# Two pieces of a recurrence unit, emitted level by level in turn

## The chip, the cores and the metric

The kernel runs on one core of one Trainium2 chip. The metric is the device time of one execution in microseconds (us). The engines are PE (TensorE, matrix products), PEld (its weight loads), DVE (VectorE), ACT (ScalarE), POOL (GpSimd) and SP (SyncE, which issues most transfers). Each engine takes its own instructions strictly in the order in which the built program lists them.

## The reference

A two-layer backbone over 2048 latent tokens and 256 context tokens of width 1024. Layer 0 is a neighbourhood attention, layer 1 a bidirectional gated linear recurrence with 8 heads of width 128. The change lies in layer 1:

```python
q, i_lat, f_fwd, f_bwd, g = jnp.split(h @ w_in, 5, axis=-1)
def step(S, inp):                                  # one chunk of tokens, per head
    A = jnp.cumsum(ac, axis=2)                     # running log decay
    o_inter = einsum('bhtk,bhkv->bhtv', qc * exp(A), S)
    scores = einsum('bhtk,bhsk,bhtsk->bhts', qc, kc, exp(rel))
    o_intra = einsum('bhts,bhsv->bhtv', scores, vc)
    S_new = exp(A_last)[..., None] * S + einsum('bhsk,bhsv->bhkv', kc * exp(A_last - A), vc)
x = x + gate * hgrn_readout(o_f + o_b, g, head_norm_w, w_out)
```

All of it is in float32 and is done for both directions, the latent scans starting from the context's final state.

## The kernel before, in words

Layer 1 has the 2048 tokens in four pieces of 512. Two pieces are resident at a time as transposed, normalised activations (`h1h`, `h1l`): pieces 0 and 1 first, then 2 and 3. A *unit* is one head on one pair of pieces, so there are 16 units: `first[0..7]` with pieces 0 and 1 (and the context), `second[0..7]` with pieces 2 and 3.

Every unit has two sections. `products` multiplies the activations with five weight granules: two forget gates, values, queries and the output gate. A granule is loaded (`g_raw`), split on ACT into `g_wh` (line 64) and on POOL into `g_wl` (line 67), and for each piece 24 matmuls of 512 columns go to one PSUM tile `g_ps` (lines 208 to 210); the context has 24 of 256 columns.

`rest` then calls `heavy` once for each piece. `heavy` computes the chunk scores with a tree of 7 levels, of blocks of 1, 2, 4, ..., 64 tokens. A first clump of 8 matmuls uses the sum of both directions' keys (`ksum`, line 918 on POOL). In each of levels 0 to 5 ACT copies the mixed keys to `km` (line 926), PE does 8 matmuls of 64 by 64 (line 914, tile `lv`; each is two passes in the trace, so 16 rows), DVE puts the result into `pm` under a mask (line 928, COPY_PREDICATED). Then `level_up` multiplies the keys (line 871), the queries (line 875) and the totals `F` (line 876) on DVE, which the next level reads. Level 6 has its own 8 matmuls (lines 933 and 934). After the levels comes the tail of the piece: transposed keys (`trp`, line 857), states (`u_ps`, line 884), outputs (`o_ps`, lines 949 and 952) with a chain of four state updates on DVE (line 954), and three stores on POOL's queue (`s_lo`, `s_lq`, `s_lu`, lines 964 to 969). `light` later walks the backward states of a second unit over all four pieces (lines 981 to 1008), reading those stores back.

In `rest` the two pieces of a unit are emitted one after the other: all levels and the tail of the first, then those of the second. The text of the program is not the order on the engines: a scheduler places the instructions of each engine by priority (what was emitted earlier goes first) and by when its model of the engines thinks that operands and buffers are there. So the levels of one unit end up between the `g_ps` products of the next unit. The helper `run` takes generators and advances them in turn until all have ended. The pieces share the score tiles' PSUM banks (`lv`, 2), the `km` buffers (2), one PSUM bank `o` for outputs and one buffer `op` for what is stored.

At the seam, `build` makes the activations of pieces 2 and 3 (lines 1047 to 1079). At the end, the last unit's `rest(2, 3)` comes before its gate granule (48 matmuls), and then `layer1_out` projects the result (`y_ps`).

Of the kernel before, what the change touches and what calls it, by code (L numbers as in the profile page):

```python
# [44 lines left out]
def custom(ap, dims, off=0):  # L45
    return bass.AP(tensor=ap.tensor, offset=ap.offset + off, ap=[list(ap.ap[0])] + dims)


class Core:
# [855 lines left out]
    def heavy(self, hd, piece, f2, k2, q2, q, v, wk, pp, sp, scale, kept, o_tag):  # L905
        nc, S = self.nc, self.S
        T = 512

        def scores(kt, qv):
            ps = pp.tile([P, 4, 64], F32, name="lv", tag="lv")  # L910
            for c in range(4):
                for u in range(2):
                    o = c * P + u * 64
                    nc.tensor.matmul(ps[64 * u:64 * u + 64, c, :], kt[:, o:o + 64], qv(o, u), start=True, stop=True)  # L914
            return ps
        pm = wk.tile([P, 4, 64], F32, name="pm", tag="pm")
        ksum = wk.tile([P, T], F32, name="ksum", tag="km")
        nc.gpsimd.tensor_add(ksum, k2[:, 0, :], k2[:, 1, :])
        ps = scores(ksum, lambda o, u: q[:, o:o + 64])
        nc.scalar.mul(out=pm, in_=ps, mul=scale)  # L920
        tot = f2
        for j in range(7):
            b = 1 << j
            if b < 64:
                km = wk.tile([P, T], F32, name="km", tag="km")
                nc.scalar.copy(out=km.rearrange("p (k h i) -> p k h i", h=2, i=b), in_=self.mixed(k2, T, b))  # L926
                ps = scores(km, lambda o, u: custom(q2, [[2 * b, 32 // b], [T + b, 2], [1, b]], o))
                nc.vector.copy_predicated(pm, self.masks[:, j, :].unsqueeze(1).broadcast_to([P, 4, 64]), ps)  # L928
            else:
                ps = pp.tile([P, 4, 64], F32, name="lv", tag="lv")  # L930
                for c in range(4):
                    o = c * P
                    nc.tensor.matmul(ps[0:64, c, :], k2[:, 0, o:o + 64], q2[:, 1, o + 64:o + P], start=True, stop=True)
                    nc.tensor.matmul(ps[64:P, c, :], k2[:, 1, o + 64:o + P], q2[:, 0, o:o + 64], start=True, stop=True)  # L934
                p = wk.tile([P, 4, P], F32, name="pf", tag="pf")
                nc.scalar.copy(out=p[0:64, :, 64:P], in_=ps[0:64])
                nc.scalar.copy(out=p[64:P, :, 0:64], in_=ps[64:P])
                nc.gpsimd.tensor_copy(p[0:64, :, 0:64], pm[0:64])
                nc.gpsimd.tensor_copy(p[64:P, :, 64:P], pm[64:P])
            nxt = self.totals(wk, T, j + 1, "F") if j < 6 else self.totals(sp, T, 7, "F")  # L940
            self.level_up(T, b, tot, k2, q2, nxt)
            tot = nxt
        nc.gpsimd.tensor_copy(self.fb[:, hd, piece, :], tot[:, 1, :])
        uf = self.states_in(k2, v, T, 0, wk, pp)
        o_ps = pp.tile([P, 4, P], F32, name="o_ps", tag=o_tag)
        s = self.sf[:, hd, :]
        last = None
        for c in range(4):
            m = nc.tensor.matmul(o_ps[:, c, :], p[:, c, :], v[:, c, :], start=True, stop=False)
            if last is not None:  # L950
                self.after(m, last)
            last = nc.tensor.matmul(o_ps[:, c, :], q2[:, 1, c * P:(c + 1) * P], s, start=False, stop=True)
            new = sp.tile([P, P], F32, name="s", tag="s") if c < 3 else self.sf[:, hd, :]
            nc.vector.scalar_tensor_tensor(new, s, tot[:, 0, c:c + 1], uf[:, c, :], ALU.mult, ALU.add)
            s = new
        if kept is None:
            op = wk.tile([P, 4, P], F32, name="op", tag="op", bufs=1)
        else:
            op, us = (kept[:, i].rearrange("p (c t) -> p c t", c=4) for i in range(2))
        nc.scalar.copy(out=op, in_=o_ps)  # L960
        if kept is not None:
            nc.scalar.copy(out=us, in_=self.states_in(k2, v, T, 1, wk, pp))
            return
        nc.gpsimd.dma_start(out=S["lo"][hd, piece], in_=op)
        nc.gpsimd.dma_start(out=S["lq"][hd, piece], in_=q2[:, 0, :])
        ub = self.states_in(k2, v, T, 1, wk, pp)
        us = wk.tile([P, 4, P], F32, name="us", tag="op", bufs=1)
        nc.scalar.copy(out=us, in_=ub)
        nc.gpsimd.dma_start(out=S["lu"][hd, piece], in_=us)
# [41 lines left out]
    def layer1(self, h1, hpool, gp):  # L1011
        nc, tc, I, S = self.nc, self.tc, self.I, self.S
        scale = float(P) ** -0.5
        with ExitStack() as st:
            wk = st.enter_context(tc.tile_pool(name="gk", bufs=2, reuse_waits="tile"))
            sp = st.enter_context(tc.tile_pool(name="gs", bufs=4, reuse_waits="tile"))
# [6 lines left out]
            pp = Banks()  # L1023
# [56 lines left out]
            class Unit:  # L1080
# [53 lines left out]
                    granule(32 + un.hd, pieces, un.o_g, nc.gpsimd if len(pieces) > 1 else nc.vector)  # L1134

                def rest(un, *pieces, o_tag="o"):
                    for g in pieces:
                        both = None
                        if un.keep:
                            both = wk.tile([P, 2, 512], F32, name="both", tag="k2", bufs=4)  # L1140
                            un.kept.setdefault(g, [None] * 3)[:2] = un.q2[g][:, 0, :], both
                        self.heavy(un.hd, g, un.f2[g], un.k2[g], un.q2[g], un.q[g], un.v[g], wk, pp, sp, scale, both, o_tag)

                def light(un, o_tag="o"):
                    return self.light(un.hd, wk, pp, sp, sm, un.kept, o_tag)
# [9 lines left out]
            def run(*work):  # L1155

                work = list(work)
                while work:
                    work = [w for w in work if next(w, work) is not work]
# [176 lines left out]
```

## Time and profile before

| | us |
|---|---|
| median of 3 runs (3338.64 to 3343.32) | 3340.88 |
| the profiled execution, its own time | 3345.1 |
| its span (first to last instruction) | 3343.3 |
| PE busy | 3211.4 |
| DVE busy | 1938.3 |
| ACT busy | 1137.0 |
| POOL busy | 842.8 |

Layer 1 begins at about 1710 us; the recurrence's clumps `lv` run from 1754.7 us to 3134 us. How to read it: busy time counts computing instructions alone. Matmuls are pipelined, so a row of the timeline gives a start and a duration, and the time that a matmul costs in a dense stream is the distance from its start to the next start, not its duration. Idle time in brackets stands in front of the instruction that waited, with what released it.

### The profile page before, as it was taken

To read this page: it belongs to the slowest core of one execution; us is meant where nothing else is said; L and a number is where in the kernel's file an instruction comes from. 1 tells how busy PE (TensorE), PEld (TensorE's weight loads), DVE (VectorE), ACT (ScalarE), POOL (GpSimd) and SP (SyncE) were. 2 spreads that over 40 slices of the span, in tenths; PEclk is the share of its full clock that TensorE was granted. 3 is DMA by queue.
4 is the path that set the end of the run, shared out by engine and by line. 5 is a ranking of instruction groups with operands and counts; after the bars stand their busy time and mean duration, and the time that the engine had idled before them with its cause. 6 is when DMAs were issued, how large, how long until landed. Compare 5 with 4: busy or idle time off the path is not lost. (4 is left out here: it accounts for less than half of the span.)

```text
span 3343.3 us, 58063 instructions
## 1 busy us (share of the span) xinstructions
PE 3211.4 (96%) x22988; PEld 2671.5 (80%) x22988; DVE 1938.3 (58%) x4002; ACT 1137.0 (34%) x2361; POOL 842.8 (25%) x813
## 2 busy tenths in 40 slices
PE   7999999999998998999999999999899999999798
PEld 4778889989787777778888888888688777887687
DVE  7674111111276776767536555565775677777776
ACT  3311110110254555553123333333533444444421
POOL 2210110110022322353322222222442323232321
PEclk8999999999999999999999999999999999999899
DMA  6566231332477767644321111112322333333543
GB/s 231 173 213 196 95 100 62 100 101 88 145 207 198 203 198 202 183 147 139 133 82 48 52 57 53 52 58 86 98 87 82 111 111 119 119 117 103 167 145 111
DMA packets 231048, 415.24 MB, mean 124 GB/s; under 512 B 35020, under 2 KB 110828, under 8 KB 230776
## 3 DMA queue, kind: packets, MB, share of 16 engines
q1 hardware_dynamic: 206904, 344.22, 33.7%
q0 software_dynamic: 23872, 67.31, 5.9%
q8 instruction: 182, 2.98, 0.4%
q14 instruction: 90, 0.74, 0.1%
HBM read 285.78 MB, written 127.10 MB: 123 GB/s over the span
## 5 line engine op out<-in xcount | busy, mean ns | idle before, releaser
L208 PE MATMUL g_ps<-h1h,g_wh 128*128 128x512 f32 x1280 | 513.9, 401 | 5.1 <-DVE qt L1094 2.5
L210 PE MATMUL g_ps<-h1h,g_wl 128*128 128x512 f32 x1280 | 511.6, 400 | 0.0
L209 PE MATMUL g_ps<-h1l,g_wh 128*128 128x512 f32 x1280 | 510.5, 399 | 0.0
L209 PE MATMUL mm<-lo,wh 128*128 128x512 f32 (+1 forms) x960 | 354.6, 370 | 1.2 <-DVE lo L202 1.0
L210 PE MATMUL mm<-hi,wl 128*128 128x512 f32 (+1 forms) x960 | 353.1, 369 | 1.3 <-POOL wl L67 1.3
L208 PE MATMUL mm<-hi,wh 128*128 128x512 f32 (+1 forms) x960 | 350.1, 371 | 1.6 <-DVE st L263 0.6
L586 DVE CUSTOM_DVE_ANT_0 p<-s,tab 128x768 f32<-128x768 f32 (+2 forms) x288 | 230.3, 836 | 122.1 <-PE s L580 101.6
L208 PEld LDWEIGHTS g_ps<-h1h,g_wh 128*128 128x128 f32 x1280 | 242.1, 189 | 56.7 <-DVE qt L1094 2.8
L210 PEld LDWEIGHTS g_ps<-h1h,g_wl 128*128 128x128 f32 x1280 | 242.2, 189 | 51.8
L67 POOL TENSOR_TENSOR g_wl<-g_raw,g_wh 128x1024 fp32r<-128x1024 f32 x86 | 209.7, 2438 | 290.7 <-ACT g_wh L64 277.8
L209 PEld LDWEIGHTS g_ps<-h1l,g_wh 128*128 128x128 f32 x1280 | 242.3, 189 | 49.2
L587 ACT ACTIVATE p<-p,nm 128x768 f32<-128x768 f32 (+2 forms) x288 | 239.8, 835 | 56.2 <-DVE nm L586 55.4
L928 DVE COPY_PREDICATED pm<-masks,lv 128x256 f32<-128x256 int32 x192 | 85.6, 446 | 262.8 <-PE lv L914 262.6
L208 PEld LDWEIGHTS mm<-hi,wh 128*128 128x128 f32 x960 | 179.8, 189 | 37.0 <-issue 2.6
L210 PEld LDWEIGHTS mm<-hi,wl 128*128 128x128 f32 x960 | 181.1, 189 | 32.3 <-POOL wl L67 1.8
L209 PEld LDWEIGHTS mm<-lo,wh 128*128 128x128 f32 x960 | 181.3, 189 | 32.1 <-DVE lo L202 2.4
L601 PE MATMUL tps<-ident,p 128*128 128x128 f32 x1472 | 198.9, 284 | 0.0
L67 POOL TENSOR_TENSOR wl<-wraw,wh 128x1024 fp32r<-128x1024 f32 x24 | 57.8, 2408 | 539.8 <-ACT wh L64 516.1
L871 DVE TENSOR_TENSOR k<-k,F 128x512 f32<-128x512 f32 (+1 forms) x240 | 165.6, 692 | 40.3 <-PE lv L934 35.6
L926 ACT COPY km<-k 128x512 f32<-128x512 f32 x192 | 129.1, 673 | 164.7 <-PE lv L914 146.0
L875 DVE TENSOR_TENSOR q<-q,F 128x512 f32<-128x512 f32 x192 | 184.6, 962 | 0.0
L601 PEld LDWEIGHTS tps<-ident,p 128*128 128x128 f32 x1472 | 164.1, 144 | 20.2 <-issue 1.5
(267 smaller groups left out, 6808.6 us busy)
## 6 DMA issues: line engine op xcount, KB each, us to landing
g_raw<-in_w SPq DMA_DIRECT2D x90, 512.0 KB
wraw<-in_w SPq DMA_DIRECT2D x32, 512.0 KB
s_q<-st SPq DMA_DIRECT2D x32, 512.0 KB
s_k<-st SPq DMA_DIRECT2D x32, 512.0 KB
adaw<-in_ada_w SPq DMA_DIRECT2D x64, 256.0 KB
q<-s_q SPq DMA_DIRECT2D x32, 512.0 KB
vb<-s_v SPq DMA_DIRECT2D x128, 128.0 KB
k<-s_k SPq DMA_DIRECT2D x16, 768.0 KB
```

The costliest lines, as they stand in the source:

```text
L67: e_lo.tensor_sub(lo, src, hi.bitcast(F32))
L208: nc.tensor.matmul(ps, wh(dc), hh(dc), start=dc == 0, stop=False)
L209: nc.tensor.matmul(ps, wh(dc), hl(dc), start=False, stop=False)
L210: m = nc.tensor.matmul(ps, wl(dc), hh(dc), start=False, stop=dc == n - 1)
L586: nc.vector.tensor_tensor_reduce(p[:, :n], s[a][:, 512 - nk:768], t, 1.0, 3.0e38, ALU.add, ALU.min, nm)
L587: core.exp = nc.scalar.activation(p[:, :n], p[:, :n], AF.Exp, bias=nm, scale=-1.0, accum_out=R.sums[:, a, j:j + 1])
L601: pin(nc.tensor.transpose(ps[:, i, :], self.p[a][:, c * P:(c + 1) * P], ident))
L871: nc.vector.tensor_mul(kv, kv, kf)
L875: nc.vector.tensor_mul(qv, qv, qf)
L926: nc.scalar.copy(out=km.rearrange("p (k h i) -> p k h i", h=2, i=b), in_=self.mixed(k2, T, b))
L928: nc.vector.copy_predicated(pm, self.masks[:, j, :].unsqueeze(1).broadcast_to([P, 4, 64]), ps)
```

## The change

`heavy` becomes a generator that yields in each level, after the level's scores are masked into `pm` and before `level_up`. `rest` makes one generator for each piece and gives them to `run`, so that level 0 of the first piece is emitted, then level 0 of the second, then `level_up` and level 1 of the first, and so on; the two tails follow at the end, first piece first. With one piece in `rest` nothing is interleaved. No instruction is added or left out. All later line numbers move by 1 and, from `rest` on, by 4.

```diff
@@ heavy
             nxt = self.totals(wk, T, j + 1, "F") if j < 6 else self.totals(sp, T, 7, "F")
+            yield
             self.level_up(T, b, tot, k2, q2, nxt)
@@ rest
+
+                    work = []
                     for g in pieces:
...
-                        self.heavy(un.hd, g, un.f2[g], un.k2[g], un.q2[g], un.q[g], un.v[g], wk, pp, sp, scale, both, o_tag)
+                        work.append(self.heavy(un.hd, g, un.f2[g], un.k2[g], un.q2[g], un.q[g], un.v[g], wk, pp, sp, scale, both, o_tag))
+                    run(*work)
```

PE, in the middle of the first eight units, before. `q_19905` are the queries of piece 0 of one unit, `q_19937` those of its piece 1; `g_ps` are products of the next unit:

```order
L208 MATMUL g_ps<-h1h,g_wh 128x512
L209 MATMUL g_ps<-h1l,g_wh 128x512
L210 MATMUL g_ps<-h1h,g_wl 128x512
L884 MATMUL u_ps<-t_v,t_kT 128x128 x2
L857 MATMUL trp<-ident,k_19530 128x128 x2
L914 MATMUL lv<-q_19905,km 64x64 x8
L208 MATMUL g_ps<-h1h,g_wh 128x512
L209 MATMUL g_ps<-h1l,g_wh 128x512
```

One level of one piece stands alone among the products here. The same unit in the changed program:

```order
L208 MATMUL g_ps<-h1h,g_wh 128x512
L209 MATMUL g_ps<-h1l,g_wh 128x512
L210 MATMUL g_ps<-h1h,g_wl 128x512
L208 MATMUL g_ps<-h1h,g_wh 128x512
L914 MATMUL lv<-q_19905,km 64x64 x8
L914 MATMUL lv<-q_19937,km 64x64 x8
L209 MATMUL g_ps<-h1l,g_wh 128x512
L210 MATMUL g_ps<-h1h,g_wl 128x512
L208 MATMUL g_ps<-h1h,g_wh 128x512
```

The clump of piece 1 has moved up beside the clump of piece 0: one interruption of the products in place of two.

DVE, the same unit, before: the level of one piece (mask, queries, keys) and between the levels work of the next unit.

```order
L928 COPY_PREDICATED pm<-masks,lv 128x256
L875 TENSOR_TENSOR q_19905<-q_19905,F_20029 128x128x2x2
L1109 TENSOR_TENSOR sgg<-g_ps,sgg 128x512
L871 TENSOR_TENSOR k_19532<-k_19532,F_20061 128x32x2x8
L928 COPY_PREDICATED pm<-masks,lv 128x256
L875 TENSOR_TENSOR q_19905<-q_19905,F_20045 128x64x2x4
```

DVE at the same levels, in the changed program:

```order
L928 COPY_PREDICATED pm<-masks,lv 128x256
L875 TENSOR_TENSOR q_19905<-q_19905,F_20029 128x128x2x2
L928 COPY_PREDICATED pm<-masks,lv 128x256
L875 TENSOR_TENSOR q_19937<-q_19937,F_20055 128x128x2x2
L871 TENSOR_TENSOR k_19532<-k_19532,F_20071 128x64x2x4
L871 TENSOR_TENSOR k_19534<-k_19534,F_20087 128x64x2x4
```

DVE now does both pieces' steps of a level in one group before the next pair of clumps can run.

PE near the end of layer 1, in the changed program: levels of the last unit (`q_30207` piece 2, `q_30239` piece 3) with the tail of the unit before it (`q_29315`) between them. In the old program this stretch holds levels of piece 2 alone, and those of piece 3 come later, among the last gate products.

```order
L914 MATMUL lv<-q_30239,km 64x64 x8
L884 MATMUL u_ps<-t_v,t_kT 128x128 x4
L914 MATMUL lv<-q_30207,km 64x64 x8
L857 MATMUL trp<-ident,k_29075 128x128 x4
L914 MATMUL lv<-q_30239,km 64x64 x8
L884 MATMUL u_ps<-t_v,t_kT 128x128 x4
L953 MATMUL o_ps<-s,q_29315 128x128
L950 MATMUL o_ps<-t_v,pf 128x128
L914 MATMUL lv<-q_30207,km 64x64 x8
```

All levels of the last unit now come ahead of its 48 gate products, and both pieces' tails come behind these.

## Rows read from the trace of the kernel before

**Rows 1.** The page's first part: busy time, share of the span, instructions.

```profile
PE 3211.4 (96%) x22988; PEld 2671.5 (80%) x22988; DVE 1938.3 (58%) x4002; ACT 1137.0 (34%) x2361; POOL 842.8 (25%) x813
```

**Rows 2.** Busy time by stretch: length, PE, PEld, DVE, ACT, POOL, granted clock, DMA.

```profile
1755.00:2340.00 585.00, 579.56 (x4428) 482.38 (x4425) 343.69 (x652) 202.40 (x376) 152.82 (x137) 1.00 0.18 58
2340.00:2460.00 120.00, 105.11 (x728) 84.90 (x727) 93.12 (x136) 60.00 (x101) 55.31 (x43) 0.94 0.30 92
2460.00:3071.50 611.50, 600.80 (x4386) 489.44 (x4385) 426.20 (x977) 256.00 (x618) 179.61 (x170) 0.99 0.34 107
3071.50:3143.90 72.40, 55.66 (x546) 46.79 (x545) 60.12 (x114) 34.19 (x73) 26.61 (x22) 0.88 0.47 151
```

**Rows 3.** Timeline of PE: start, duration, instruction; one clump among products.

```profile
2343.02 0.39 PE L210 MATMUL g_ps<-h1h,g_wl 128*128 128x512 f32 x1
2343.34 0.69 PE L914 MATMUL lv<-q,km 128*64 128x64 f32 x16
2343.96 0.50 PE L208 MATMUL g_ps<-h1h,g_wh 128*128 128x512 f32 x1
2344.29 0.39 PE L209 MATMUL g_ps<-h1l,g_wh 128*128 128x512 f32 x1
2344.52 0.40 PE L210 MATMUL g_ps<-h1h,g_wl 128*128 128x512 f32 x1
```

**Rows 4.** Timeline of PE, two clumps side by side among products.

```profile
1961.54 0.39 PE L209 MATMUL g_ps<-h1l,g_wh 128*128 128x512 f32 x1
1961.86 0.27 PE L933 MATMUL lv<-q,k 128*64 128x64 f32 x1
...
1962.38 0.64 PE L914 MATMUL lv<-qt,ksum 128*64 128x64 f32 x16
1962.94 0.50 PE L210 MATMUL g_ps<-h1h,g_wl 128*128 128x512 f32 x1
1963.28 0.39 PE L208 MATMUL g_ps<-h1h,g_wh 128*128 128x512 f32 x1
```

**Rows 5.** Timeline of PE, ten passes of 128 columns among products.

```profile
2004.06 0.39 PE L208 MATMUL g_ps<-h1h,g_wh 128*128 128x512 f32 x1
2004.28 0.38 PE L949 MATMUL o_ps<-t_v,pf 128*128 128x128 f32 x2
...
2005.31 0.48 PE L209 MATMUL g_ps<-h1l,g_wh 128*128 128x512 f32 x1
2005.62 0.39 PE L210 MATMUL g_ps<-h1h,g_wl 128*128 128x512 f32 x1
```

**Rows 6.** Groups of DVE, 1755 to 2340 us: count, busy, mean ns, idle before.

```profile
L875 DVE TENSOR_TENSOR q<-q,F 128x512 f32<-128x512 f32 x80 | 82.5, 1031 | 0.0
L871 DVE TENSOR_TENSOR k<-k,F 128x512 f32<-128x512 f32 x81 | 61.9, 764 | 13.7 <-PE lv L934 12.4 <-ACT km L926 1.3
L928 DVE COPY_PREDICATED pm<-masks,lv 128x256 f32<-128x256 int32 x81 | 36.3, 448 | 159.5 <-PE lv L914 159.5
```

**Rows 7.** Line 875 on DVE, 1755 to 2340 us: ns min/median/max.

```profile
L875 DVE TENSOR_TENSOR q<-q,F x80: 672/681/2925, 1762.9 to 2338.1; 128x512 f32<-128x512 f32 x80
```

**Rows 8.** Timeline of DVE and, in the second fence line, of POOL.

```profile
2338.14 2.92 DVE L875 TENSOR_TENSOR q<-q,F 128x512 f32<-128x512 f32 x1
2338.12 2.40 POOL L67 TENSOR_TENSOR g_wl<-g_raw,g_wh 128x1024 fp32r<-128x1024 f32 x1 [0.89 <-ACT g_wh L64]
```

**Rows 9.** Groups of POOL, 1755 to 2340, then 2460 to 3071.5 us.

```profile
L67 POOL TENSOR_TENSOR g_wl<-g_raw,g_wh 128x1024 fp32r<-128x1024 f32 x34 | 83.2, 2446 | 126.9 <-ACT g_wh L64 121.7 <-PE g_ps L210 4.9
L67 POOL TENSOR_TENSOR g_wl<-g_raw,g_wh 128x1024 fp32r<-128x1024 f32 x37 | 89.6, 2422 | 118.3 <-ACT g_wh L64 115.8 <-PE o_ps L952 2.3
```

**Rows 10.** Waits of PE, 2340 to 2460 us: total us, times, longest.

```profile
PE lv L914 <- DVE brs L174: 5.5, 1, 5.5
PE lv L933 <- DVE q L875: 4.2, 1, 4.2
```

**Rows 11.** Waits of PE, 3071.5 to 3143.9 us.

```profile
PE lv L914 <- DVE q L875: 5.1, 4, 2.1
PE lv L914 <- DVE rq_t L172: 2.7, 1, 2.7
```

**Rows 12.** What ACT waited for ahead of line 968, whole trace: us, times.

```profile
DMA s_lo<-op: 34.7, 19
```

## Prediction, made before the changed kernel ran

> **What bounds the kernel now.** I read the page's busy times first, then the busy time by stretch of layer 1, then PE's waits in the stretches where it idles, and last PE's timeline at a few clumps. The reader is to see that PE is the bound: it is busy 96% of the span [rows 1], and between 1755 and 2340 us, where the first eight units run, 579.56 of 585 us, with DVE at 344 and ACT at 202 [rows 2]. Only 5.4 us of that stretch, and 10.7 us of the 611.5 between 2460 and 3071.5, are PE idle. So there a better order can gain little by ending waits; it can gain only if PE's own stream gets shorter. PE does idle at the seam where pieces 2 and 3 are built (14.9 of 120 us) and at the end of layer 1 (16.7 of 72.4 us) [rows 2]. At the end DVE, with 60.1 of 72.4 us, is nearer its limit than PE.
>
> **What a clump costs PE.** Products follow each other at 0.23 us (2344.29 to 2344.52). From the last product before a lone clump to the second product behind it 1.27 us pass (2343.02 to 2344.29); two product steps would be 0.46, so a lone clump of 16 passes costs 0.81 us [rows 3]. A double clump of 32 passes takes 1.74 us between the same points (1961.54 to 1963.28), so it costs 1.28 us [rows 4]. Two lone clumps cost 1.62, and **joining two saves 0.34 us** of PE's time. It is paid in three places: the first pass starts 0.32 us after the last product and not 0.23, the first product starts late, and the second product 0.33 us after the first.
>
> It is the change to 64 columns that is dear, not any change of work: ten passes of 128 columns put among products take 1.56 us from product to second product (2004.06 to 2005.62); less two product steps that is 1.10 us, or 0.11 a pass, and nothing for the change [rows 5]. So I count clumps of `lv`, not all changes of work. The Trainium skill, "TensorEngine Tiling (Array Packing)", section Key Properties, says that changing the tiling mode, not merely the tile, drains TensorE. By that rule every entry to and exit from a 128 by 64 clump pays and a move between the 128 by 128 kinds does not, which is what these rows show; a sum over all changes of work would count twice as many as pay.
>
> **How many are joined.** The order of PE's instructions in the two programs gives the runs of `lv` matmuls that nothing interrupts. From the first clump to the first transposes of the seam there are 112 before and 63 now; in the seam 12 and 12; from there to the end of the last unit's products 132 and 123; after that 16 and 13. In the second half the walk over the backward states (`light`) cuts pairs apart again, hence the small change.
>
> **The change part by part**, against the profiled execution's 3345.1 us (span 3343.3):
>
> - First half: 49 joined × 0.34 = 16.7 us less on an engine that is 99% busy.
> - Second half: 9 × 0.34 = 3.1 us less.
> - New waits in these two halves. PE now needs both pieces' steps at one point. A pair needs 2 × (1.03 + 0.76 + 0.45) = 4.5 us of DVE, by means that hold DVE's delays already [rows 6]; in the place shown 21 products stand between two pairs, 4.8 us, and the pair itself takes 1.1. That covers it, with 1.4 us to spare, but before the change one piece's 2.2 us stood against about as many products. What else DVE does, 56% overall [rows 2], falls in part into the same interval. Bounds: 0, as now, up to the 39 us of the slower rival below. I take 5 us, a third more than the 16 us of idle time that the two stretches have, because the means of DVE stay under the interval.
> - Tails. In the old order the tail of the first piece was spread among the second piece's levels; now both tails follow each other: `op` has one buffer, so the copies and stores of the two pieces form one chain, store by store. ACT already waits for `s_lo`, 34.7 us in 19 times, 1.8 us each [rows 12], and key copies stand behind that wait. 15 units have both pieces here and one more such wait each: 15 × 1.8 = 27 us of ACT at most, off PE's path as long as products stand behind it. ACT is 35% busy [rows 2]; I add nothing and leave the bound to the range. SP's and POOL's transfers keep their number; each store moves with its tail.
> - The seam. Its two long waits are a level of the last first-half unit that stands behind the chain of the new pieces' normalisation on DVE (5.5 us) and a level-6 clump (4.2 us) [rows 10]. In the new order all levels of that last interleaved unit are ahead of the transposes, but the next unit's first level takes such a place. Bounds 0 and 9.7 us; I take 4.
> - The end. Before, no products stand in 3071.5 to 3103.5 us, 32 us, in which piece 2 of the last unit does its seven levels; then 40.4 us with 48 gate products and piece 3's levels, with waits of 5.1 and 2.7 us in the whole [rows 11]. Now both pieces do 14 levels in the first part. Its DVE work is 14 × 2.2 = 31 us by the means, and the tail of the unit before some 9 us more, so 40 us (8 more). The second part is then 48 × 0.23 = 11 us of products and two tails, about 13 us by what stands between 3131 and 3143.9 now: 24 us, 16 less. Together 8 less. Bounds: 0, and 16, since DVE's 60 us [rows 2] less some 4 us (two or three of its level steps now run earlier) have to fit.
>
> Sum: −16.7 − 3.1 + 5 − 4 − 8 = −26.8 us, 3318.3 us for the profiled execution. That execution is 4.2 us above the median of the runs, 3340.88; so **3314 us** in the measure of the runs.
>
> **The rivals.**
>
> 1. *DVE is held by POOL, and the change is slower.* A query step on DVE takes 0.68 us in the median and up to 2.93 [rows 7]; the one at 2338.14 took 2.92 us while POOL's 2.40 us subtraction for a granule ran from 2338.12 [rows 8]. There are 34 and 37 of these subtractions in the two halves [rows 9]. Until now such a hold hit one piece with a spare of 2 to 3 us before its next clump; now it pushes both pieces of a pair, whose spare is 1.4 us, and PE stands in front of the pair with its products queued behind. It costs PE about 1 us when it hits a pair's steps in full. The saving of 31.8 us is used up from 0.45 us for each of the 71; at 0.55, or 39 us, the sum is +7: **3348 us**, slower. For it: PE cannot pass the pair. Against it: the interval of 5.9 us is above the 4.5 us that already include the mean hold. The Trainium skill, "SBUF — State Buffer", section "SBUF: two separate sides", states that DVE and GpSimd share a port pair by an exclusive lock held for a whole instruction. By that rule the hold cannot be shared away and every subtraction that overlaps a pair costs in full; the 2.92 us row agrees.
> 2. *Waits eat the joined clumps; no change.* The same place at about 0.4 us for each subtraction, or the ACT waits of the tails at their bound of 27 us: the sum is within 6 us of zero, **3340 us**.
> 3. *Only the clumps count.* At the seam the wait merely changes its owner, and at the end 14 uncovered levels take as long as before in all: −16.7 − 3.1 + 5 = −14.8, **3326 us**. For it: at the end DVE is the nearer limit, and its work does not shrink.
>
> That the order does not change is excluded by the order itself: 49 pairs stand side by side in the first half.
>
> **How the numbers follow.** Forecast 60% (its own range 3298 to 3329); only the clumps 18%; no change 13%; slower 9%. What a measurement of this kernel can tell from no change is 0.2%, 6.7 us: below 3334.2 is faster, above 3347.6 slower. Faster 0.78, same 0.13, slower 0.09. The range from 3296 to 3336 leaves out the slower rival, about half of the no-change one and a twentieth below, where the end gains all of its 16 us and the seam all of its 9.7.
>
> **What would show it.** In the changed profile PE's busy time in the first half's stretch should fall by about 17 us with idle still under 10; double clumps of 32 passes should stand among products at 1.28 us each. The row of the end should be some 64 us long and the seam's two long waits smaller. DVE's, ACT's and POOL's busy times should stay. I am wrong if the first half is as long as before, with `lv` waiting for `q` some 20 us more; then the pairs wait, and rival 1 or 2 holds. I am wrong in size if the joined clumps do not take 1.28 us, or if the end stays at 72 us.

## The result, and the profile after

The changed kernel takes **3304.74 us** in the median (3296.95 to 3306.53, 4 runs) against 3340.15 for the kernel before in the same set; the ratio is 0.9884, with a 95% interval from 0.9869 to 0.9900. The forecast was 3314, in a range of 3296 to 3336. The sign and the cause of the largest term came out as forecast. The second half, the seam and the projection gained more than forecast and the end lost where a gain was forecast, and these misses partly offset each other.

The profiled execution took 3304.15 us, 41.0 less than the one before. Of that 6.1 us lie ahead of layer 1: its first product starts at 1682.75 instead of 1688.86. In layer 0 the two traces run within some 1.5 us of each other up to about 0.9 ms; behind that the distance comes and goes with PE's waits in the attention (between 1000 and 1600 us 14.3 us in one and 8.2 in the other for `q<-s_q`, but 10.1 and 16.9 for `ot`). Over all profiled executions of this study that start lies between 1679.2 and 1693.6 us, so it says nothing on the change, and all that follows counts from it. From there to the start of the last `y_ps` it is 1644.5 us before and 1609.7 now: 34.9 less, which is what the medians say (35.4).

Busy time by stretch in the changed kernel, cut at the same instructions as [rows 2], with the projection `y_ps` as a fifth row. Columns as there.

```profile
1748.89:2320.28 571.39, 560.96 (x4452) 475.33 (x4449) 333.71 (x652) 202.46 (x375) 154.97 (x135) 1.00 0.17 59
2320.28:2430.10 109.82, 102.64 (x704) 83.88 (x703) 86.06 (x136) 60.95 (x103) 55.91 (x45) 1.00 0.32 106
2430.10:3031.00 600.90, 593.79 (x4420) 486.67 (x4419) 426.54 (x974) 253.51 (x616) 182.41 (x173) 1.00 0.34 109
3031.00:3107.00 76.00, 57.76 (x522) 49.65 (x521) 52.09 (x121) 34.42 (x84) 19.88 (x18) 0.85 0.43 137
3107.00:3292.60 185.60, 182.41 (x822) 149.97 (x821) 144.31 (x357) 50.91 (x128) 45.28 (x19) 1.00 0.43 146
```

Length by length: 585.0 to 571.4 us (PE busy 18.6 us less, idle 5.0 more), 120.0 to 109.8, 611.5 to 600.9, but the end 72.4 to 76.0. The projection's stretch of before is a row that was not shown:

```profile
3143.90:3333.60 189.70, 184.47 (x832) 152.36 (x831) 141.34 (x361) 50.36 (x134) 41.26 (x18) 0.98 0.41 139
```

A joined pair in the first half, on PE's timeline of the changed kernel. The clump has the shape of [rows 4], from one more place:

```profile
1948.61 0.39 PE L210 MATMUL g_ps<-h1h,g_wl 128*128 128x512 f32 x1
1948.93 1.15 PE L914 MATMUL lv<-q,km 128*64 128x64 f32 x32
1950.01 0.50 PE L208 MATMUL g_ps<-h1h,g_wh 128*128 128x512 f32 x1
1950.35 0.39 PE L209 MATMUL g_ps<-h1l,g_wh 128*128 128x512 f32 x1
```

From 1948.61 to 1950.35 it is 1.74 us; less two product steps, 1.28 us, the forecast's price to the hundredth. There is one entry and one exit for the 32 passes of both pieces.

PE's waits in the first half (1748.89 to 2320.28) of the changed kernel: total us, times, longest.

```profile
PE lv L933 <- DVE q L875: 6.9, 5, 1.4
PE trp L857 <- ACT vT L850: 2.4, 5, 0.5
PE trp L857 <- DVE k L871: 1.1, 1, 1.1
```

The `km` levels (line 914) wait for nothing; before, it was 0.4 us once. Only level 6 (line 933) waits, five times. It uses keys and queries straight from `level_up`, without ACT's copy between; whether that is why was not tested.

The end shows the one new long wait. PE, then DVE, then POOL and SP, in the changed kernel around 3060 us; idle time ahead of an instruction stands in brackets:

```profile
3062.51 0.60 PE L857 MATMUL trp<-ident,vT 128*128 128x128 f32 x4
3070.21 2.45 PE L989 MATMUL o_ps<-s,box 128*128 128x128 f32 x8 [7.11 <-DVE s L992]
3072.31 0.78 PE L208 MATMUL g_ps<-h1h,g_wh 128*128 128x512 f32 x1
```

```profile
3059.98 0.88 DVE L875 TENSOR_TENSOR q<-q,F 128x512 f32<-128x512 f32 x1
3069.80 0.35 DVE L992 SCALAR_TENSOR_TENSOR s<-sb,fb,box 128x128 f32<-128x128 f32 x1 [8.94 <-DMA box<-s_lu]
```

```profile
3064.67 0.54 POOL L970 DMA_DIRECT2D s_lu<-us  x1 [2.70 <-ACT us L969]
3067.23 0.32 SPq L984 DMA_DIRECT2D box<-s_lu  x1
```

```profile
3061.43 0.54 POOL L965 DMA_DIRECT2D s_lo<-op  x1 [0.31 <-ACT op L961]
3063.73 0.32 SPq L985 DMA_DIRECT2D box<-s_lo  x1
3063.79 0.59 ACT L969 COPY us<-u_ps 128x512 f32<-128x512 f32 x1
```

Line 989 is the backward walk of unit 6. Its first state step on DVE (line 992) reads the states that this unit's second tail stored: the store is issued at 3064.67, the load at 3067.23, and the step starts at 3069.80. That is 5.1 us from store to use, while all levels of the last unit are done (DVE's last ended at 3060.9) and its 48 gate products stand on PE behind the walk. The last fence shows what stands ahead of the store: the outputs of the same tail are stored first, from the one `op` buffer that `us` takes next, and the copy into `us` starts as the load that follows that store is issued.

The Trainium skill, "SBUF — State Buffer", section "The DMA setup-cost knee", fits the time of a transfer by about 2 us and its bytes at 436 GB/s, and calls the fit an approximation. By that page the 256 KB store and the load that waits for it take 2.6 us each, an estimate of 5.2 us; the trace agrees with 5.1, of which 2.56 lie between the two issues.

### The profile page after: what moved, and what is told of

Read it like the earlier page. It is cut to its first block, busy times and chain, and to the rows that moved or that the text cites. A ratio compares the mean times of both kernels' runs of the same rounds, so it can differ in the third digit from the quotient of the medians.

```text
span 3302.3 us, 58252 instructions
## 1 busy us (share of the span) xinstructions
PE 3178.0 (96%) x22988; PEld 2657.8 (80%) x22988; DVE 1916.1 (58%) x4002; ACT 1136.8 (34%) x2361; POOL 845.6 (26%) x813
## 5 line engine op out<-in xcount | busy, mean ns | idle before, releaser
L208 PEld LDWEIGHTS g_ps<-h1h,g_wh 128*128 128x128 f32 x1280 | 241.2, 188 | 49.8 <-DVE hf L1076 0.6
L208 PE MATMUL mmv<-vh,hi 128*128 128x256 f32 x576 | 163.0, 283 | 0.0
L209 PE MATMUL mmv<-vl,hi 128*128 128x256 f32 x576 | 163.0, 283 | 0.0
L210 PE MATMUL mmv<-vh,lo 128*128 128x256 f32 x576 | 163.0, 283 | 0.0
```

Of the source, the lines that this page charges most:

```text
L208: nc.tensor.matmul(ps, wh(dc), hh(dc), start=dc == 0, stop=False)
L209: nc.tensor.matmul(ps, wh(dc), hl(dc), start=False, stop=False)
L210: m = nc.tensor.matmul(ps, wl(dc), hh(dc), start=False, stop=dc == n - 1)
```

## The experiments

The table gives the stage lengths of every profiled execution in us, each the difference of two starts on PE's timeline: first `lv` to the seam's first transpose; to its last; to the last product ahead of the last gate; to the first `y_ps`; to the last `y_ps`. The seam's cuts lie 25 us behind the first and 20 us ahead of the second of those in [rows 2]. The sixth column adds the last two stages, the seventh runs from layer 1's first product to the last `y_ps`.

| | first half | seam | second half | end | `y_ps` | end + `y_ps` | layer 1 |
|---|---|---|---|---|---|---|---|
| before | 610.3 | 75.0 | 631.4 | 72.6 | 189.5 | 262.1 | 1644.5 |
| changed | 592.8 | 68.5 | 620.9 | 76.2 | 185.4 | 261.6 | 1609.7 |
| e1_first | 592.8 | 68.5 | 629.1 | 73.9 | 189.6 | 263.5 | 1619.7 |
| e2_second | 611.0 | 73.7 | 619.4 | 69.8 | 186.0 | 255.9 | 1625.8 |
| e3_last | 610.7 | 75.1 | 631.7 | 70.2 | 188.4 | 258.6 | 1641.9 |
| e4_not_last | 592.7 | 68.5 | 619.8 | 70.0 | 189.1 | 259.1 | 1605.9 |
| e5_gate_early | 592.7 | 68.5 | 619.8 | 84.6 | 182.3 | 266.9 | 1613.7 |
| e6_light_late | 592.7 | 69.4 | 617.6 | 84.5 | 180.4 | 264.9 | 1610.3 |
| e10_l6_o | 593.1 | 68.7 | 618.2 | 75.9 | 202.5 | 278.4 | 1624.3 |
| e13_notlast_l6o | 593.0 | 68.5 | 619.5 | 78.6 | 197.4 | 276.0 | 1622.8 |
| e14_other | 592.9 | 68.6 | 621.5 | 64.5 | 188.7 | 253.2 | 1602.0 |
| e16_usfirst | 592.5 | 72.8 | 617.5 | 62.4 | 186.5 | 248.9 | 1597.6 |
| e17_usfirst6 | 592.9 | 68.5 | 617.8 | 67.8 | 189.9 | 257.7 | 1602.8 |
| e18_usfirst6_notlast | 592.8 | 68.5 | 619.5 | 68.2 | 190.6 | 258.8 | 1605.4 |

The first half repeats within 0.6 us over all of those that share its edit, so its gain is known well. The second half repeats less well: nine kernels have the very same order of PE's instructions there (the changed one, e4 to e14, e17 and e18) and take 617.6 to 621.5 us. Of the last two stages there are only two runs with nearly the old kernel's order, which differ by 1.4 us in their sum.

**Which stage gains.** Four kernels apply the change to some units only, by a condition in `rest`:

```diff
-                    run(*work)
+                    if 0 in pieces:
+                        run(*work)
+                    else:
+                        for w in work:
+                            run(w)
```

This is e1_first; e2_second has `2 in pieces and not un.keep`, e3_last `un.keep`, e4_not_last `not un.keep`.

> Only the units of the first half (pieces 0 and 1) have their two pieces' levels in turn; the second half and the last unit go piece by piece as before. PE's order is that of the changed kernel through the seam, and behind it that of the kernel before. Theory A (each stage has its own gain, and what it gains stays): the first half is 17 us shorter with 49 joined clumps and the seam 6 us, so 23 to 24 us less than before, 3317. Theory B (the gain of the first half is only shifted, and the second half, bound by its own waits, gives part of it back): less than 15 us.

Measured: 3318.81 us against 3341.6, ratio 0.9922 (0.9909 to 0.9936), 22.8 us less. The first half is 17.5 us shorter and the seam 6.5, and the second half does not give it back. Theory A holds.

> Only units 0 to 6 of the second half have their levels in turn; the first half and the last unit go piece by piece. The prediction's own price (9 clumps less of lv at 0.34 us, and idle time about as before) gives 3 us less than before. Theory A, from the changed kernel's stage times (631.4 to 620.9 us between the seam and the last products): 10 us less, 3330, since what counts is how often PE changes between lv and any other work, products above all, and idle time of PE falls by 4 us too.

Measured: 3326.18 us, ratio 0.9950 (0.9937 to 0.9962), 15.4 us less. The second half is 12.0 us shorter: theory A, and not the forecast's 3 us. The end and the projection are 6.2 us shorter too, which neither expected.

> Only the last unit has its levels in turn. The prediction's step for the end: 8 us less than before, all of it between the last products of the unit and the first y_ps. Theory A: nothing gained, within 2 us of before, or some us more: with both pieces' levels done early, nothing is left for PE while the backward walk waits for the stored states of the unit before, and the gate products stand behind that walk.

Measured: 3338.30 us, ratio 0.9989 (0.9981 to 0.9998); the last two stages are 3.5 us shorter. The forecast's 8 us are not there; theory A's bound of 2 us is passed as well. So the last unit alone does gain something when the unit before it goes piece by piece.

> All units but the last have their levels in turn; the last goes piece by piece. The prediction's step for the end: 8 us slower than the changed kernel, 3313. Theory A (the end gains nothing by the change, and piece 3's levels still cover the wait for the stored states): as long as the changed kernel or up to 5 us shorter, 3300 to 3305.

Measured: 3303.46 us, ratio 0.9887 (0.9872 to 0.9902). To leave the last unit out costs nothing, where the forecast's step would have cost 8 us. In this kernel the stored states are waited for by DVE for 1.7 us instead of 8.9, since piece 3's levels stand there, and PE's wait ahead of the walk is short:

```profile
3068.89 0.54 POOL L970 DMA_DIRECT2D s_lu<-us  x1 [3.72 <-ACT us L969]
3074.26 0.35 DVE L992 SCALAR_TENSOR_TENSOR s<-sb,fb,box 128x128 f32<-128x128 f32 x1 [1.68 <-DMA box<-s_lu]
```

```profile
PE o_ps L989 <- DVE s L992: 0.8, 1, 0.8
```

The first row is POOL's timeline, the second DVE's, the third PE's waits between the last products and the first `y_ps`. From store to use it is 5.4 us here too: as long as in the changed kernel, but covered.

**Can other work fill the wait?** Three kernels move the gate products or the walk.

```diff
 e5_gate_early
+            second[7].gate(2, 3)
             next(l6), next(l6)
             second[7].rest(2, 3)
-            second[7].gate(2, 3)
             next(l6), next(l6)
 e6_light_late
-            next(l6), next(l6)
             second[7].rest(2, 3)
             second[7].gate(2, 3)
-            next(l6), next(l6)
+            next(l6), next(l6), next(l6), next(l6)
 e10_l6_o
-            l6, l7 = second[6].light("mm"), second[7].light()
+            l6, l7 = second[6].light(), second[7].light()
```

> The changed kernel, with the last unit's 48 gate products emitted ahead of the backward walk of the unit before; in PE's order they stand ahead of all but the first of the last unit's levels. Round-trip theory (in the changed kernel PE waits 7.1 us at that walk for states that were stored only 5 us before, with the gate products queued behind): the wait falls under the levels, and the products fill PE's gaps ahead of it; but nothing is then left for the tails. 5 us less than the changed kernel, 3300. Rival (the end is bound by DVE's level steps): same as the changed kernel within 2 us, since the levels only start later.

Measured: 3304.93 us, ratio 0.9899 (0.9885 to 0.9912): no gain, and by the trace the last two stages are 5.3 us longer than in the changed kernel. The walk's wait falls to 4.9 us in three, but levels without products beside them now wait, 9.1 us in six (`lv` for `q`):

```profile
PE lv L914 <- DVE q L875: 9.1, 6, 2.8
PE o_ps L989 <- DVE s L992: 4.9, 3, 3.1
```

> The changed kernel, with the backward walk of unit 6 emitted behind the last unit and its gate products; in PE's order the products then stand among the levels, and the whole walk of both units behind the tails. Round-trip theory: the 7.1 us wait goes, the products hide under the levels; but 16 steps of the walk with nothing beside them, about 0.75 us each, stand ahead of the first y_ps: between 3 us less and 5 us more than the changed kernel. Rival (DVE's level steps bound the end): 5 to 12 us more, by the walk alone.

Measured: 3310.03 us, ratio 0.9911 (0.9898 to 0.9925), 5.3 us more by the medians and 0.7 by layer 1's length. The walk's wait is 1.0 us, but the first `y_ps` waits 9.9 us in one piece, behind a walk with nothing beside it. By the medians that is at the slow edge of what the round-trip theory gave and the fast edge of its rival's; it does not decide.

> The changed kernel with one word changed: the walk of unit 6 takes its PSUM tile from bank o and not from the banks that the products use. Nothing else is moved by hand. Round-trip theory, with its cause (the products cannot pass the walk because their PSUM buffers come after the walk's in turn): the products move by themselves among the levels, the 7.1 us wait goes, and the first y_ps come among the last tails: 8 to 12 us less than the changed kernel, 3293 to 3297. Rival (DVE's level steps bound the end): within 3 us of the changed kernel.

Measured: 3324.64 us, ratio 0.9958 (0.9944 to 0.9971), 20 us **more** by the medians and 14.6 by layer 1's length. My expectation was wrong by 30 us, in sign too. The order did what I said: the products moved among the levels by themselves. But the wait did not go with them. PE at the walk in this kernel:

```profile
3085.77 1.65 PE L989 MATMUL o_ps<-s,box 128*128 128x128 f32 x6 [9.41 <-DVE s L992]
```

The walk's states come 55.8 us behind the last product of the units and not 39.4, PE waits for them for 9.4 us, and with the products gone only the tails and the projection are behind it; the end is as long as before the edit (75.9), the projection 17 us longer. The walk comes later because the store that it reads does:

```profile
3079.83 0.56 POOL L970 DMA_DIRECT2D s_lu<-us  x1
```

That is 49.8 us behind the last product of the units, 33.8 in the changed kernel, and 5.5 us ahead of the walk's step on DVE (3085.36). With the gate products out of the way, ACT's casts and POOL's subtractions for the weights of `y_ps` (`h1h` and `h1l` from `wor`) moved up too: eight of each stand ahead of that store, none in the changed kernel. Whether they are what delays it was not tested. So this run does not tell what the 48 products alone are worth: the wait was still there.

e13_notlast_l6o has this edit together with the condition of e4_not_last.

> As the run with all units but the last interleaved (3303.5), with the walk of unit 6 in PSUM bank o. It tells whether the last unit should be interleaved once nothing holds the products. If joined clumps of the last unit save nothing there because PE is not the bound: as long as the same change with all units interleaved, within 2 us. If the levels of both pieces in turn give DVE and PE a shorter chain: 5 us more than that.

Measured: 3321.88 us, ratio 0.9941 (0.9929 to 0.9954), 2.8 us less than with all units interleaved, by the trace 1.4. Whether the last unit is interleaved makes no clear difference there either.

**Take the wait itself away.** In e14_other the walk reads another unit's stored data, in place of moving anything:

```diff
+                src = 5 if hd == 6 and piece > 1 else hd
-                nc.sync.dma_start(out=ub, in_=S["lu"][hd, piece])
+                nc.sync.dma_start(out=ub, in_=S["lu"][src, piece])
```

The loads of `lq` and `lo` have the same edit.

> The changed kernel, except that the backward walk of unit 6 reads, for pieces 2 and 3, the stored queries, states and outputs of unit 5 (the same loads and the same work, with values that were stored long before; the results for that head are other numbers). PE's order at the end is that of the changed kernel but for a few places. Round-trip theory: the 7.1 us wait of PE for the walk's states goes, and with it the end is 5 to 7 us shorter: 3298 to 3300. Rival (the end is bound by the last unit's own levels and tails, the wait only stands where PE would have idled anyway): within 2 us of the changed kernel.

Measured: 3293.88 us, ratio 0.9859 (0.9843 to 0.9876), 10.9 us less than the changed kernel's median and 8.3 by the two ratios, each against the old kernel in its own set. The end is 64.5 us instead of 76.2; end and projection together are 8.4 us shorter, and the stages ahead of them are as they were. PE's waits for the walk's states at the end (7.3 us before this edit) and the end's busy row, 3029.6 to 3093.9 us:

```profile
PE o_ps L990 <- DVE s L993: 1.8, 2, 1.4
```

```profile
3029.60:3093.90 64.30, 52.40 (x521) 44.92 (x520) 51.45 (x117) 34.34 (x82) 20.64 (x18) 0.97 0.47 152
```

The rival, that PE would have idled there anyway, falls: PE's idle time at the end is 11.9 us instead of 18.2, and its busy time falls too, at a granted clock of 0.97 instead of 0.85. That 64.5 us is the 64 that the forecast named for the end is luck, as the account below shows.

**Store earlier.** In the tail, the backward states can be computed and stored ahead of the forward outputs:

```diff
+        def back():
+            nc.gpsimd.dma_start(out=S["lq"][hd, piece], in_=q2[:, 0, :])
+            ub = self.states_in(k2, v, T, 1, wk, pp)
+            us = wk.tile([P, 4, P], F32, name="us", tag="op", bufs=1)
+            nc.scalar.copy(out=us, in_=ub)
+            nc.gpsimd.dma_start(out=S["lu"][hd, piece], in_=us)
+        if kept is None:
+            back()
         uf = self.states_in(k2, v, T, 0, wk, pp)
```

with the same five lines removed behind the outputs. e16_usfirst does it in all units; e17_usfirst6 only in unit 6 of the second half; e18_usfirst6_notlast adds that to e4_not_last.

> The changed kernel, with each tail's backward states computed and stored ahead of its forward outputs, in all units. Round-trip theory: the last stored states of unit 6 come back earlier, so the 7.1 us wait at the walk goes and the end is some 5 us shorter, 3300, if the other stages stay. Rival: the forward states, which the next unit's tails do not need but DVE's queue holds, come later, the wait moves to the outputs, and nothing is gained.

Measured: **3294.89 us** (3288.56 to 3298.64), ratio 0.9859 (0.9839 to 0.9878). This is the fastest kernel here that leaves nothing out, about 10 us under the changed one by the medians, 8 by the ratios and 12 by layer 1's length. Its seam is 4.3 us longer, the second half 3.4 and the end 13.7 us shorter.

> The same edit in unit 6 of the second half alone, so that all stages ahead of the end keep the changed kernel's order. Round-trip theory: 5 us less than the changed kernel, 3300, all of it between the last products and the end. Rival as above: within 2 us of it.

Measured: 3296.77 us, ratio 0.9870 (0.9850 to 0.9889). The end is 67.8 us instead of 76.2. The store is issued at 3053.19 and the walk's step starts at 3058.10, 4.9 us later. The last unit's levels still run over most of that, so DVE waits 1.4 us and not 8.9:

```profile
3053.19 0.54 POOL L951 DMA_DIRECT2D s_lu<-us  x1
```

```profile
3058.10 0.35 DVE L998 SCALAR_TENSOR_TENSOR s<-sb,fb,box 128x128 f32<-128x128 f32 x1 [1.39 <-DMA box<-s_lu]
```

By the medians this is 8 us; by the ratios it is 4.7, and their intervals overlap. By layer 1's length it is 6.9, of which 3.9 at the last two stages, since the projection is 4.5 us longer, and 3.0 in the second half. PE's order there did stay, as expected, and 617.8 us lies among the lengths of the other kernels with that order, so the 3.0 are not put down to the edit.

> The run with all units but the last interleaved (3303.5), with the same edit in unit 6. There the walk waits under 1 us already, so by the round-trip theory nothing is gained: within 2 us of that run. Rival (states stored earlier help the walk by themselves, wherever it stands): 3 to 5 us less.

Measured: 3303.97 us, ratio 0.9887 (0.9870 to 0.9902), as e4_not_last (3303.46). Where the wait was covered, an earlier store gains nothing. At the last two stages the same edit is worth 3.9 us with the wait bare (261.6 to 257.7) and 0.3 with it covered (259.1 to 258.8).

## Why the prediction was right, and where not

**First half, −16.7: right.** By its own cuts (first clump to the seam's transposes) the stage is 17.4 us shorter, with PE's busy time down 16.9 (599.3 to 582.4); a pair costs 1.28 us as priced. e1_first gives 17.5 by itself. By these cuts the old stretch holds the 5.5 us wait that [rows 10] and the forecast put at the seam; with that wait gone and the new ones added its idle time is much as before (11.0 us, now 10.4), so that the shortening is PE's busy time alone.

**New waits, +5: right in sum in the first half, wrong in the second.** PE's idle time between the cuts of [rows 2] rose from 5.4 to 10.4 us in the first. In the second half it fell, from 10.7 to 7.1: there the old order had two waits of a level for its queries, 4.5 and 1.6 us; in the changed order no level of that stretch waits for them at all.

**Second half, −3.1: the term mis-sized.** It is 10.6 us shorter. 3.1 are the 9 clumps, 3.6 are idle time. Other kernels with these two orders agree: 629.1 to 631.7 us in the old one, 617.6 to 621.5 in the new. A third piece is the clock behind waits. In the old kernel, after the 4.5 us wait:

```profile
2615.64 1.12 PE L914 MATMUL lv<-q,km 128*64 128x64 f32 x16 [4.52 <-DVE q L875]
2616.70 2.08 PE L988 MATMUL o_ps<-s,box 128*128 128x128 f32 x8
...
2619.00 0.63 PE L209 MATMUL g_ps<-h1l,g_wh 128*128 128x512 f32 x1
2619.42 0.63 PE L210 MATMUL g_ps<-h1h,g_wl 128*128 128x512 f32 x1
```

The granted clock of 2612 to 2622 us is 0.66, and products follow each other at 0.43 us, nearly twice the 0.23 of the full level: the lower of the clock's two levels. Eleven product steps of this stretch are so long in the old kernel and four in the new, 1.4 us less. The clump and the eight passes ahead of them ran at that level too. PE's work at a granted clock of 0.50, the first two rows from the old second half and the third from the new:

```profile
2615.64:2620.39 4.75, 4.75 (x29) 4.25 (x30) 4.75 (x11) 3.61 (x13) 0.00 (x0) 0.50 0.56 177
2709.13:2712.55 3.42, 3.42 (x8) 2.77 (x9) 3.42 (x9) 2.34 (x4) 1.51 (x1) 0.50 0.53 153
```

```profile
2842.40:2845.81 3.41, 3.41 (x14) 2.54 (x11) 2.41 (x7) 0.96 (x3) 1.25 (x3) 0.50 0.51 193
```

If all of it ran at half the pace, the old order lost 4.1 us by it and the new one 1.7, an estimate of 2.4 us less. The 1.5 of the 10.6 us that remain are within what this stretch varies by. The failed step is the assumption that idle time stays as it was: the forecast counted the change's own risk of waits and not the waits that the old order already had.

**The seam, −4: the right cause, too small.** Between the cuts of [rows 2], from which the forecast took it, the stretch is 10.2 us shorter (120.0 to 109.8), more than the 9.7 that were its bound; 7.7 of it are idle time. By the table's cuts, which leave the first of the two long waits to the first half, it is 6.5. The 5.5 us wait of a level behind the normalisation's chain is gone, and so is the 4.2 us wait of level 6. Waits at the transposes, 1.1 us in two before, are now

```profile
PE tp L1074 <- DVE hf L1076: 4.3, 5, 1.5
```

e1_first has it all.

**The end, −8: wrong.** The stretch of 72.4 became 76.0, and with the projection the sum is 0.5 us less. Both parts of it were sized wrongly. The changed kernel's first part, then its 48 products, then the rest up to the first `y_ps`, as in the rows above (length, PE, PEld, DVE, ...):

```profile
3030.83:3072.31 41.48, 28.47 (x366) 24.35 (x365) 31.26 (x70) 17.27 (x35) 6.99 (x11) 0.86 0.32 103
3072.31:3085.28 12.97, 12.97 (x59) 10.68 (x59) 8.81 (x26) 6.21 (x23) 3.31 (x2) 0.92 0.27 82
3085.28:3106.99 21.71, 16.48 (x101) 14.77 (x99) 12.01 (x27) 11.10 (x26) 9.57 (x6) 0.80 0.74 234
```

The first part took 41.5 us to the first gate product, 40 forecast, but not by what was forecast: DVE did 31.3 us of work in it, not 40, and waited 8.9 us for the stored states, PE 7.1 us for DVE. The forecast counted PE's and DVE's work and left out the walk over unit 6's states, which stands ahead of the gate products, needs what the last tail of unit 6 stored, and ran under piece 3's levels in the old order. With both pieces' levels early and both tails late, the 5.1 us from store to use had nothing beside it. The chain of stores through the one `op` buffer, which the step on the tails put at nothing, stands ahead of it. e14_other and e17_usfirst6 show the wait: with it away the last two stages are 8.4 and 3.9 us shorter.

The second part took 34.7 us, 24 forecast: 13.0 for the products (11), 12.8 for the two tails (13, from 3088.83 to 3101.66), and 8.9 for more of the walks, 3.6 of it between the products and the tails and 5.3 ahead of the first `y_ps`, which the forecast left out as well. In e14_other the two parts, cut in the same way, are 31.8 and 32.7 us. So its 64.5 us meet the forecast's 64 by two misses of 8 to 9 us that cancel.

**Rivals.** Rival 1 falls: the query steps between two levels did not grow under POOL's subtractions, they shrank. The means of [rows 6] and the spread of [rows 7], in the changed kernel's first half:

```profile
L875 DVE TENSOR_TENSOR q<-q,F 128x512 f32<-128x512 f32 x82 | 65.2, 795 | 0.0
```

```profile
L875 DVE TENSOR_TENSOR q<-q,F x82: 657/683/1531, 1760.4 to 2315.9; 128x512 f32<-128x512 f32 x82
```

A query step is 795 ns in the mean, 1031 before, and 1.53 us at most, 2.93 before. POOL's subtractions are as many and as long (34 of 2.43 us): they fall elsewhere. Added up from the starts and ends of all these steps, they ran beside a subtraction for 20.1 us before and for 4.7 now. All that took over 0.9 us, 22 before and 13 now, ran beside some POOL instruction. So the holds did not go; they moved, in part to the first query step of a unit, which grew:

```profile
L875 DVE TENSOR_TENSOR q<-q,f 128x512 f32<-128x512 f32 x14 | 17.5, 1251 | 5.6 <-PE lv L914 5.6
L875 DVE TENSOR_TENSOR q<-q,f 128x512 f32<-128x512 f32 x14 | 22.6, 1613 | 5.6 <-PE lv L914 5.6
```

The first row is before, the second the changed kernel; DVE's busy time in the stretch fell from 343.7 to 333.7 us all the same. I had taken the old means as given in a new order. Rival 2's ACT waits did not come either: ACT's waits for `s_lo` ahead of line 968 were 34.7 us [rows 12]; ahead of the same copy, now line 969, they are

```profile
ACT us L969 <- DMA s_lo<-op: 19.5, 12, 5.4
```

Rival 3 (only the clumps) named the end's fate rightly, nothing gained there, with a different reason.

One reading of the prediction is off and carries nothing: DVE's share in the first half by [rows 2] is 59%, and 70% in the second, not 56%.

The sum by the cuts of [rows 2], forecast in brackets: −13.6 in the first half (−16.7 and its part of the +5), −10.2 at the seam (−4), −10.6 in the second half (−3.1 and its part of the +5), +3.6 at the end (−8), −4.1 in the projection (none). That is −34.9 against −26.8. The end missed by 11.6 us one way and the other terms together by 19.7 the other way, so that the total came within 8 us is partly luck.

## What to carry to other kernels

Where an engine is full, count how often its stream changes kind, price one change from start-to-start distances, and join what can stand side by side: in the first half that part held to 5%. When steps are moved earlier, ask which wait they used to cover: the states that the last tail of unit 6 stores were used 4.9 us or more after the store's issue in every kernel here that reads them back, and a late tail makes that wait bare. Before moving work into a gap, take the gap's cause away in a trial; moving the 48 products or the walk gained nothing in three placements, taking the wait away gained 8 us, and storing one tile earlier some 4 us at the last two stages.

## What was not expected of the hardware

A DVE step of one shape had a mean of 1031 ns in one order and 795 in another, with the same median of 0.68 us and as many subtractions on POOL. Every one of these steps over 0.9 us ran beside a POOL instruction, so a mean read in one order is not a price in another. And PE's two waits of 4.5 and 1.6 us in the old second half were each followed by work at a granted clock of 0.50, for 4.8 and 3.4 us: by the estimate above the wait cost about half to a whole of itself again.
